# An encoder block on one core: the order of Down's loads, of the norm2 transposes and of the first loads of x

## The chip, the core and the metric

The kernel is one launch on one core of a Trainium2 chip. The core has a matrix engine (TensorE, "PE" in the profile, its weight loads "PEld"), a vector engine (DVE), a scalar engine (ACT), GpSimd (POOL) and a queue engine (SP) that only issues DMAs. POOL also issues some DMAs. Each engine runs its own instructions strictly in the order in which the program lists them; semaphores tie the engines together. The metric is device time in microseconds (us), lower is better.

## The reference, cut to what matters

```
def reference(x, ...):                      # x: 1 x 1024 rows x 1024 channels, float32
    xn = rmsnorm(x, norm1)
    x  = x + token_mixer(xn, ...)           # mLSTM (4 heads, two directions) and
                                            # differential attention (8 heads):
                                            # y = sigmoid(ga)*(h_a @ p_a) + sigmoid(gb)*(h_b @ p_b)
                                            # return y @ w_o
    x  = x + conv_ffn(rmsnorm(x, norm2), ...)
def conv_ffn(xn, w_up, conv_w, conv_b, w_down):
    u = conv3(xn @ w_up) + conv_b           # 1024 -> 5632 channels, 3 taps along the rows
    a, g = split(u, 2)
    return (gelu(g) * a) @ w_down           # 2816 -> 1024
def rmsnorm(x, g): return x * rsqrt(mean(x*x) + 1e-6) * g
```

## The kernel before

All arithmetic is float32. For the matrix engine each operand is split into a high part (rounded to the engine's fp32r) and a low remainder, and a product is three matmuls, high x high, low x high, high x low (`mm3`, lines 101 to 103). The high part is a cast on ACT (L81), the low part a subtraction on DVE (L83) or POOL (L88). So every tile that enters a product costs ACT and DVE or POOL an instruction before PE may start.

The stages, in the order in which PE meets them:

1. **Start.** x is loaded in eight blocks of 128 rows (512 KB each), in two halves of four blocks: half 0 on SP's queue, half 1 on POOL's queue (L273). `norm_transpose` normalises a half: square with a row sum on ACT (L233), scale and add on DVE (L220), power -1/2 on POOL (L221), scaling of the rows on DVE (L236). Then PE transposes the rows in 128 x 128 pieces (L242), ACT evicts them as high part (L243) and DVE as low part (L244) of xn, and the first projections (tile `pj`) follow.
2. **mLSTM**, **attention** and **merge**, not touched by the change.
3. **w_o** (tile `sm`, weights `whi`/`wlo`, left operand `y`, 128 x 256 pieces). `wo_piece` multiplies two blocks of rows with 256 columns: 48 matmuls, and DVE adds the residual (L985). The first twelve of sixteen pieces complete rows 0 to 3 (of eight blocks). `norm0` then normalises these four blocks (`rows(0, ...)`: squares L1049, L220, L221, scaling L1055), transposes them (`turn`, L1061) into the blocks A11 and A12, and evicts each transposed piece three times: high part on ACT (L1076), low part on DVE (L1077), an unsplit copy `f` on ACT (L1078). Then come the last four w_o pieces, for rows 4 to 7, and norm1, the same for these rows.
4. **Up**: x1n @ w_up by a Strassen-Winograd scheme with seven products for each of 22 column blocks j, then the convolution, GELU and gate. The results go to DRAM: `h_d` 0 and 1 by POOL's queue (L1238, L1240), the pair sums `h_d` 2 and 3, formed by DVE (L1251 to L1254), by SP's queue (L1255, L1256).
5. **Down**: the same scheme, seven products n = 0..6, each over 11 steps kk. A step needs a 512-wide piece of h (`hr`, loaded in pairs of kk, L1336) and of w_down (`wd`: n = 0 loads the even row blocks, n = 1 the odd ones, L1304), splits both (`dh` on ACT, `dl` on DVE) and runs 12 matmuls. For n = 1, 2 and 6 DVE forms weight sums first (L1323 to L1328). `x1r` is the residual (L1367).

Tiles live in rings: a tag names a ring with a fixed count of buffers, and a new tile waits for the last user of the buffer that it takes. The ring "A" holds the blocks A11, A12 and their sums in Up, and then parts of w_down and t3 in Down; "B" and "acc" hold rows, `hr`, `x1r`, and the other part of w_down.

The order on each engine is not the order of the code: a scheduler simulates the program at build time and lists each engine's instructions as they come ready in its own model of time. `tc.issue_after(ins)` adds an edge to this: what is issued inside may not be listed ahead of `ins`.

Of the kernel before, what the change touches and what calls it, by code (L numbers as in the profile page):

```python
# [39 lines left out]
NH = 4  # L40
PRO = 4
LAST = (2, 2, 2, 2, 0, 0, 0, 0)
TURN0 = {1: (0,), 2: (2, 3)}
# [7 lines left out]
class Kern:  # L51
# [46 lines left out]
    def mm3(self, ps, a, b, start, stop, again=False):  # L98

        mm = self.nc.tensor.matmul  # L100
        mm(ps, a[0], b[0], start=start, stop=False, skip_group_check=again)  # L101
        mm(ps, a[0], b[1], start=False, stop=False, skip_group_check=again)  # L102
        mm(ps, a[1], b[0], start=False, stop=stop, skip_group_check=again)  # L103

# [113 lines left out]
def rstd_pow(K, out, ss, n, scr, width):  # L218

    K.nc.vector.tensor_scalar(scr, ss, 1.0 / n, EPS, op0=ALU.mult, op1=ALU.add)  # L220
    K.nc.gpsimd.tensor_tensor(out, scr, K.mhalf[:scr.shape[0], :width], op=ALU.pow)  # L221


def norm_transpose(K, xb, xT, gain, tmp, half, dst, psf):


    nc = K.nc
    xs = []
    for b4 in range(4):
        x = xb(half * 4 + b4)  # L230
        ss = tmp.tile([P, 2], F32, tag="nss", bufs=8, name=K.nm("nss"))
        junk, o = dst(x)
        nc.scalar.activation(junk, x, AF.Square, accum_out=ss[:, 0:1])  # L233
        r = tmp.tile([P, 1], F32, tag="nr", bufs=8, name=K.nm("nr"))
        rstd_pow(K, r, ss[:, 0:1], D, ss[:, 1:2], 1)
        nc.vector.tensor_scalar(o, x, r, None, op0=ALU.mult)  # L236
        xs.append(o)
    t = slice(half * 512, half * 512 + 512)
    for k in range(KT):
        ps = psf(k)  # L240
        for b4 in range(4):
            nc.tensor.transpose(ps[:, b4 * P:(b4 + 1) * P], xs[b4][:, k * P:(k + 1) * P], K.ident)  # L242
        nc.scalar.activation(xT[0][k][:, t], ps, AF.Copy, scale=gain[:, k:k + 1])  # L243
        nc.vector.scalar_tensor_tensor(xT[1][k][:, t], ps, gain[:, k:k + 1],  # L244
                                       xT[0][k][:, t].bitcast(F32), op0=ALU.mult, op1=ALU.subtract)


def mlstm(K, xn, g1, gate_bias, ha_d):
# [4 lines left out]
    with tc.tile_pool(name="ml", bufs=1, reuse_waits="tile") as mp, ExitStack() as es:  # L253
# [23 lines left out]
        def norm(xs, half):  # L277
            norm_transpose(K, lambda blk: xs[blk % 4], xn, g1, mp, half,
                           lambda x: (K.big(), x), lambda k: K.small(tag="cr"))
# [614 lines left out]
def merge_ffn(K, ha_d, hb_d, out):  # L894
    nc, tc, I = K.nc, K.tc, K.I
    V, G, A, T = nc.vector, nc.gpsimd, nc.scalar, nc.tensor
    with tc.tile_pool(name="mf", bufs=1, reuse_waits="tile") as fp, ExitStack() as es:
# [99 lines left out]
        for i in range(2):  # L997
            for bp in range(2):
                wo_piece(ws[i], 2 + i, bp * 2)
        up.norm0([g4("nxs", tag="wk") for _ in range(2)] + [g4("nxs", tag="B") for _ in range(2)], lambda k: K.small())  # L1000
# [8 lines left out]
class Up:  # L1009
# [53 lines left out]
    def norm0(self, scr, psf):  # L1063
        nc, G, V = self.K.nc, self.K.nc.gpsimd, self.K.nc.vector
        xs = self.rows(0, scr)
        self.f = []
        for kk in range(4):
            f = self.g4("f", tag="acc")
            for i, name in enumerate(("11", "12")):
                k = kk + 4 * i  # L1070
                ps = psf(2 * kk + i)
                self.turn(xs, k, ps)
                h, l = self.block(name, kk, "A")
                t = slice(i * 512, i * 512 + 512)
# [4 lines left out]
            self.f.append(f)  # L1079

    def norm1a(self):
# [206 lines left out]
class Down:  # L1288
# [7 lines left out]
    def __init__(self, K, g4, up, out):  # L1296
        self.K, self.g4, self.up, self.out = K, g4, up, out
        self.e, self.o, self.t3 = [None] * self.NK, [None] * self.NK, [None] * self.NK
        self.raw = {}
# [30 lines left out]
    def act(self, n, kk):  # L1330

        if kk % 2 == 0 and (n, kk) not in self.raw:
            (i, c), m = self.ORDER[n][0], min(2, self.NK - kk)
            t = self.g4("hr", tag="B" if n == 0 and kk < 4 else "acc")
            src = self.up.h_d[i][kk * P:(kk + m) * P, c:c + 512]
            self.K.nc.sync.dma_start(t[:, :m * 512].rearrange("p (k t) -> p k t", k=m),  # L1336
                                     src.rearrange("(k p) t -> p k t", p=P))
            self.raw[n, kk] = t
# [22 lines left out]
    def x1(self, th, ch, add):  # L1361
        V, nc = self.K.nc.vector, self.K.nc
        r = []
        for b2 in range(2):
            t = self.g4("x1r", tag="B")
            r0, c = (th * 4 + b2 * 2) * P, slice(ch * 512, ch * 512 + 512)
            nc.sync.dma_start(t.rearrange("p (b c) -> p b c", b=2),  # L1367
                              self.up.x1_d[r0:r0 + 2 * P, c].rearrange("(b p) c -> p b c", p=P))
            for i in range(2):
# [123 lines left out]
```

## Time and profile before

| | |
|---|---|
| median of the runs | 2150.89 us (2146.47, 2150.89, 2152.11) |
| profiled execution, its own time | 2153.54 us |
| span of the profiled execution | 2151.8 us |
| PE busy | 2081.1 us, 97% of the span, 11808 matmuls and transposes |
| DVE, ACT, POOL busy | 1328.1, 961.8, 450.4 us |

The profiled execution's own time is 1.7 us more than its span and 2.65 us more than the median. A row of the waits says how long an engine stood idle in front of instructions of a line, in how many places, and which instruction let it go on. A row of the busy time by stretch gives for each engine the busy time and (xN) the instructions in it, then the granted clock of PE as a share of full speed, the busy share of the DMA engines, and GB/s. PE's instructions overlap, so a matmul's own duration is longer than its distance to the next one.

### The profile page before, as it was taken

The page shows a single profiled execution, that of the slowest core. Times are in us where ns is not written, and L with a number is a line of the kernel's source. Part 1 is how long each engine was busy: PE and PEld are TensorE (multiplying, and loading weights), DVE is VectorE, ACT ScalarE, POOL GpSimd, SP SyncE. Part 2 cuts the span into 40 slices and gives each one's busy share as a digit, 9 for nine tenths or more (in the row PEclk, how much of TensorE's full clock was granted, in tenths as well). Part 3 has the DMA queues.
Part 4 walks back from the last instruction along what each step waited for, and adds up shares of the span by engine and source line. Part 5 has one row for each costly group of instructions (what it writes and reads, how often), then busy time and mean ns, then how long its engine had stood idle before and what let it go on. Part 6 is the DMA issues. An engine that isn't in the chain of part 4 may idle for free.

```text
span 2151.8 us, 30492 instructions
## 1 busy us (share of the span) xinstructions
PE 2081.1 (97%) x11808; PEld 1803.0 (84%) x11808; DVE 1328.1 (62%) x2128; ACT 961.8 (45%) x1781; POOL 450.4 (21%) x557
## 2 busy tenths in 40 slices
PE   7999999999999999999999999999999999998999
PEld 5878889898889888988888888898788888887887
DVE  4356454445586856858666534425987777779554
ACT  4332222234555655645655422205645444544443
POOL 1111000143442624425240010000121222120000
PEclk9999999999999999999999999999999999999999
DMA  4224322153413325233243364512232322358441
GB/s 138 40 85 124 67 71 60 40 137 59 99 45 72 80 59 96 52 84 70 64 95 103 127 212 157 165 42 79 79 111 96 113 98 96 111 192 303 141 137 45
DMA packets 167134, 217.39 MB, mean 101 GB/s; under 512 B 18292, under 2 KB 124996, under 8 KB 166988
## 3 DMA queue, kind: packets, MB, share of 16 engines
q1 hardware_dynamic: 152492, 165.55, 25.9%
q0 software_dynamic: 14496, 49.88, 8.8%
q8 instruction: 93, 1.52, 0.3%
q14 instruction: 53, 0.43, 0.1%
HBM read 149.82 MB, written 48.79 MB: 92 GB/s over the span
## 4 chain that ended last, share of the span: by engine, by line
PE 56%; DMA 2%; DVE 2%; ACT 1%; issue 1%; SPq 0%; POOL 0%; ACTq 0%; DVEq 0%
PE sm L101 13%; PE sm L102 13%; PE sm L103 13%; PE pj L101 3%; PE pj L102 3%; PE pj L103 3%; PE big L688 2%; PE pt L719 1%; DMA kst<-st 1%; PE po L101 1%; PE po L102 1%; PE po L103 1%; DMA hr<-h_d 0%; DMA wd<-in_w_down_dram 0%; PE big L101 0%
## 5 line engine op out<-in xcount | busy, mean ns | idle before, releaser
L101 PE MATMUL pj<-whi,xn 128*128 128x256 f32 x960 | 277.6, 289 | 1.1 <-ACT raw L598 1.1
L102 PE MATMUL pj<-wlo,xn 128*128 128x256 f32 x960 | 274.9, 286 | 0.0
L103 PE MATMUL pj<-whi,xn 128*128 128x256 f32 x960 | 274.6, 286 | 0.0
L101 PE MATMUL pj<-xn,whi 128*128 128x512 f32 x512 | 210.4, 412 | 4.2 <-ACT tg L154 2.0
L102 PE MATMUL pj<-xn,whi 128*128 128x512 f32 x512 | 207.7, 406 | 0.0
L103 PE MATMUL pj<-xn,wlo 128*128 128x512 f32 x512 | 207.0, 404 | 0.0
L101 PEld LDWEIGHTS pj<-whi,xn 128*128 128x128 f32 x960 | 183.5, 191 | 5.3 <-ACT raw L598 2.0
L102 PEld LDWEIGHTS pj<-wlo,xn 128*128 128x128 f32 x960 | 183.3, 191 | 2.2
L103 PEld LDWEIGHTS pj<-whi,xn 128*128 128x128 f32 x960 | 183.3, 191 | 1.1
L694 ACT ACTIVATE p<-big,smx 128x1024 f32<-128x1024 f32 x128 | 143.3, 1120 | 82.4 <-DVE smx L692 69.7
L692 DVE TENSOR_REDUCE smx<-big 128x1 f32<-128x1024 f32 x128 | 154.6, 1217 | 39.6 <-PE big L688 39.1
L81 ACT CAST whi<-wraw 128x1024 fp32r<-128x1024 f32 x88 | 92.2, 1049 | 158.5 <-DMA wraw<-in_w_in_dram 34.9
L1234 POOL TENSOR_TENSOR cv<-cv,cv 128x256 f32<-128x256 f32 x88 | 81.5, 954 | 353.0 <-ACT uh L81 122.9
L688 PE MATMUL big<-kst,qst 128*128 128x512 f32 x512 | 145.3, 403 | 4.6 <-ACT p L694 2.4
L83 DVE TENSOR_TENSOR wlo<-wraw,whi 128x1024 fp32r<-128x1024 f32 x54 | 66.3, 1228 | 129.1 <-ACT whi L81 128.9
L102 PE MATMUL sm<-AS,uh 128*128 128x512 f32 x352 | 138.9, 395 | 0.8 <-DVE AS L83 0.8
L101 PE MATMUL sm<-AS,uh 128*128 128x512 f32 x352 | 138.6, 394 | 0.9 <-ACT AS L81 0.7
L103 PE MATMUL sm<-AS,ul 128*128 128x512 f32 x352 | 137.7, 394 | 1.5 <-DVE ul L83 1.5
L83 DVE TENSOR_TENSOR wTl<-pt,wTh 128x512 fp32r<-128x512 f32 x128 | 87.0, 685 | 80.6 <-ACT wTh L81 80.4
L88 POOL TENSOR_TENSOR wlo<-wraw,whi 128x256 fp32r<-128x256 f32 x136 | 110.7, 845 | 118.6 <-ACT whi L81 118.3
L101 PE MATMUL sm<-dh 128*128 128x512 f32 x308 | 116.1, 393 | 7.3 <-ACT dh L81 7.3
L102 PE MATMUL sm<-dl,dh 128*128 128x512 f32 x308 | 120.3, 392 | 0.0
(311 smaller groups left out, 5308.4 us busy)
## 6 DMA issues: line engine op xcount, KB each, us to landing
ur<-in_w_up_dram SPq DMA_DIRECT2D x88, 256.0 KB, 3.3
hr<-h_d SPq DMA_DIRECT2D x35, 512.0 KB, 3.8
kst<-st SPq DMA_DIRECT2D x128, 128.0 KB, 2.6
wraw<-in_w_in_dram SPq DMA_DIRECT2D x24, 512.0 KB, 5.5
h_d<-cv SPq DMA_DIRECT2D x22, 512.0 KB, 2.6
wd<-in_w_down_dram SPq DMA_DIRECT2D x22, 512.0 KB, 9.8
sig<-tg SPq DMA_DIRECT2D x32, 256.0 KB, 2.3
wraw<-in_w_in_dram POOLq DMA_DIRECT2D x16, 512.0 KB, 6.1
```

The source lines that it names most:

```text
L81: self.nc.scalar.copy(hi, src)
L83: self.nc.vector.tensor_tensor(lo, src, hi.bitcast(F32), op=ALU.subtract)
L88: lo_eng.tensor_tensor(lo[:, t], src[:, t], hi[:, t].bitcast(F32), op=ALU.subtract)
L101: mm(ps, a[0], b[0], start=start, stop=False, skip_group_check=again)
L102: mm(ps, a[0], b[1], start=False, stop=False, skip_group_check=again)
L103: mm(ps, a[1], b[0], start=False, stop=stop, skip_group_check=again)
L688: T.matmul(sps[c_][:, half * 512:half * 512 + 512], o.q[st.qp][:, c_, t], o.k[half][:, c_, s_, :], start=s_ == 0, stop=s_ == 1)
L692: V.tensor_reduce(sm[:, c_:c_ + 1], sp, op=ALU.max, axis=AX.X, negate=True)
L694: K.mark = A.activation(p_, sp, AF.Exp, bias=sm[:, c_:c_ + 1], accum_out=sm[:, 2 + c_:3 + c_]).ins
L719: T.transpose(pt[:, kk * 256 + j * P:kk * 256 + (j + 1) * P], st.w[j][:, kb * P:(kb + 1) * P], K.ident)
L1234: nc.gpsimd.tensor_tensor(a[:, t], a[:, t], g[:, t], op=ALU.mult)
```

## The change

- **Start.** 28 transposes of the identity into the PSUM tile `pj` are issued ahead of everything else on PE. x's half 1 is loaded after the last power of half 0's normalisation, so SP's four blocks come first and alone.
- **norm0** becomes a generator. Rows 0 to 3 are normalised as before, but the transposes are cut in four turns of eight, one after each of the four remaining w_o pieces, and each turn may not be listed ahead of that piece's last matmul.
- **Down.** All loads of Down (`hr`, `wd`, `x1r`) go through `ld`, which keeps them in the order in which the code issues them. Even row blocks of w_down take buffers of ring "A", odd ones of ring "B" (before: the other way round).

```
+WARM = 28
...
+        self.last_mm = mm(ps, a[1], b[0], start=False, stop=stop, skip_group_check=again).ins
...
+    return K.nc.gpsimd.tensor_tensor(out, scr, K.mhalf[:scr.shape[0], :width], op=ALU.pow).ins
...
             if first:
                 xs0 = load_x(0, nc.sync)
+                for i in range(WARM):
+                    if i % 4 == 0:
+                        ps = K.small(tag="pj")
+                    T.transpose(ps[:, i % 4 * P:i % 4 * P + P], K.ident, K.ident)
...
-                norm(xs0, 0)
-                xs1 = load_x(1, G)
+                last = norm(xs0, 0)
+                with tc.issue_after(last):
+                    xs1 = load_x(1, G)
...
-        up.norm0([g4("nxs", tag="wk") ...], lambda k: K.small())
+        turns = up.norm0([g4("nxs", tag="wk") ...], lambda k: K.small())
+        next(turns)
         for i in range(2):
             for bp in range(2):
                 wo_piece(ws[i], 2 + i, 4 + bp * 2)
+                next(turns)
...
         self.f = []
+        yield
         for kk in range(4):
...
-                self.turn(xs, k, ps)
+                with self.K.tc.issue_after(self.K.last_mm):
+                    self.turn(xs, k, ps)
...
+    def ld(self, dst, src):
+        if self.last is None:
+            self.last = self.K.nc.sync.dma_start(dst, src).ins
+        else:
+            with self.K.tc.issue_after(self.last):
+                self.last = self.K.nc.sync.dma_start(dst, src).ins
...
-        t = self.g4("wd", tag="A" if k % 2 else "B")
-        K.nc.sync.dma_start(t, K.I["w_down"][0][k * P:(k + 1) * P, :])
+        t = self.g4("wd", tag="B" if k % 2 else "A")
+        self.ld(t, K.I["w_down"][0][k * P:(k + 1) * P, :])
...
-            self.K.nc.sync.dma_start(t[:, :m * 512]...)        # hr, and x1r likewise
+            self.ld(t[:, :m * 512]..., ...)
```

Line numbers of the changed kernel are 1 higher from line 42, some 8 higher from line 290 and 10 to 20 higher behind that.

POOL's instructions at the start (`nr` the power of half 0's four blocks, `x` the loads of half 1), before:

```order
L273 DMA x_217<-in_x_dram 128x1024
L273 DMA x_219<-in_x_dram 128x1024
L273 DMA x_221<-in_x_dram 128x1024
L273 DMA x_223<-in_x_dram 128x1024
L221 TENSOR_TENSOR nr_136<-nss_133,mhalf 128x1
L221 TENSOR_TENSOR nr_143<-nss_140,mhalf 128x1
L221 TENSOR_TENSOR nr_150<-nss_147,mhalf 128x1
L221 TENSOR_TENSOR nr_157<-nss_154,mhalf 128x1
```

and after the change:

```order
L222 TENSOR_TENSOR nr_171<-nss_168,mhalf 128x1
L222 TENSOR_TENSOR nr_178<-nss_175,mhalf 128x1
L222 TENSOR_TENSOR nr_185<-nss_182,mhalf 128x1
L222 TENSOR_TENSOR nr_192<-nss_189,mhalf 128x1
L275 DMA x_252<-in_x_dram 128x1024
L275 DMA x_254<-in_x_dram 128x1024
L275 DMA x_256<-in_x_dram 128x1024
L275 DMA x_258<-in_x_dram 128x1024
```

The four loads of half 1 move behind the four powers, each of which waits for a block of half 0.

PE at the w_o pieces, where rows 0 to 3 are turned (`nxs` normalised rows). Before, the end of one piece and the first of 32 transposes, which stand in one row:

```order
L101 MATMUL sm_13981<-whi_13807,y_12796 128x256
L102 MATMUL sm_13981<-wlo_13808,y_12796 128x256
L103 MATMUL sm_13981<-whi_13807,y_12804 128x256
L1061 MATMUL sm_14065<-ident,nxs_14032 128x128
L1061 MATMUL sm_14075<-ident,nxs_14032 128x128
L1061 MATMUL sm_14086<-ident,nxs_14032 128x128
L1061 MATMUL sm_14094<-ident,nxs_14032 128x128
```

After the change, the end of the last piece, the fourth turn and the first product of Up (`A`, `uh`, `ul`):

```order
L103 MATMUL sm_14311<-wlo_13843,y_12835 128x256
L104 MATMUL sm_14311<-whi_13842,y_12843 128x256
L1071 MATMUL sm_14363<-ident,nxs_14067 128x128
L1071 MATMUL sm_14363<-ident,nxs_14068 128x128
L1071 MATMUL sm_14363<-ident,nxs_14069 128x128
L1071 MATMUL sm_14363<-ident,nxs_14070 128x128
L1071 MATMUL sm_14371<-ident,nxs_14067 128x128
L1071 MATMUL sm_14371<-ident,nxs_14068 128x128
L1071 MATMUL sm_14371<-ident,nxs_14069 128x128
L1071 MATMUL sm_14371<-ident,nxs_14070 128x128
L102 MATMUL sm_14428<-A_2146_14156,uh_14379 128x512
L103 MATMUL sm_14428<-A_2147_14157,uh_14379 128x512
```

The other three turns stand in the same way behind the first three of the last four pieces (of the first turn, two transposes stand nine matmuls into the next piece); nothing stands now between the piece that completes rows 0 to 3 and the next piece's matmuls.

SP at the seam of Up and Down, before (the last four of eleven `wd` loads in a row, then two `x1r`, then the `hr` of kk = 4):

```order
L1304 DMA wd_17871<-in_w_down_dram 128x1024
L1304 DMA wd_17893<-in_w_down_dram 128x1024
L1304 DMA wd_17913<-in_w_down_dram 128x1024
L1304 DMA wd_17935<-in_w_down_dram 128x1024
L1367 DMA x1r_18141<-x_d 128x2x512
L1367 DMA x1r_18145<-x_d 128x2x512
L1336 DMA hr_17807<-h_d 128x2x512
```

After the change (from the `hr` of kk = 2 to the `hr` of kk = 6; the two `h_d` are the stores of an earlier pair):

```order
L1320 DMA hr_17800<-h_d 128x2x512
L1320 DMA wd_17802<-in_w_down_dram 128x1024
L1320 DMA wd_17822<-in_w_down_dram 128x1024
L1268 DMA h_d<-cv_17538 128x1024
L1269 DMA h_d<-cv_17398 128x1024
L1320 DMA hr_17842<-h_d 128x2x512
L1320 DMA wd_17844<-in_w_down_dram 128x1024
L1320 DMA wd_17864<-in_w_down_dram 128x1024
L1320 DMA hr_17884<-h_d 128x2x512
```

Each `hr` now stands directly ahead of the `wd` of its own two steps; the `hr` of kk = 10 is row 332 of SP, `x1r` and the odd blocks come behind it.

DVE at the same seam after the change (`dl` the low parts of Down's steps kk = 5 to 7, L1264 to L1266 the pair sums of the last pair of Up):

```order
L84 TENSOR_TENSOR dl_17867<-wd_17864,dh_17866 128x512
L84 TENSOR_TENSOR dl_17889<-hr_17884,dh_17888 128x512
L1264 TENSOR_TENSOR cv_17758<-cv_17682,cv_17763 128x512
L84 TENSOR_TENSOR dl_17909<-hr_17884,dh_17908 128x512
L1265 TENSOR_TENSOR cv_17758<-cv_17758,cv_17682 128x512
L1266 TENSOR_TENSOR cv_17682<-cv_17682 128x512
L84 TENSOR_TENSOR dl_17889<-wd_17886,dh_17888 128x512
L84 TENSOR_TENSOR dl_17909<-wd_17906,dh_17908 128x512
```

Before the change the weight sums of n = 1 (L1323 to L1326) stood among these rows, fifteen of them ahead of PE's stop; now all 44 stand behind the last `dl` of n = 0.

## Rows read from the trace of the kernel before

**Rows 1.** PE's line of the profile page: busy, share, instructions, of all engines.

```profile
PE 2081.1 (97%) x11808; PEld 1803.0 (84%) x11808; DVE 1328.1 (62%) x2128; ACT 961.8 (45%) x1781; POOL 450.4 (21%) x557
```

**Rows 2.** Waits of PE over the whole span: for, total us, times, longest us.

```profile
PE cr L242 <- DVE x L236: 13.7, 2, 12.3
...
PE sm L101 <- ACT dh L81: 7.3, 1, 7.3
...
PE cr L461 <- DVE dn L476: 3.9, 1, 3.9
```

**Rows 3.** ACT in order of time at the start, first and last square of half 0.

```profile
7.42 1.03 ACT L233 ACTIVATE big<-x 128x1024 f32<-128x1024 f32 x1 [5.03 <-DMA x<-in_x_dram]
...
15.45 1.03 ACT L233 ACTIVATE big<-x 128x1024 f32<-128x1024 f32 x1 [1.51 <-DMA x<-in_x_dram]
```

**Rows 4.** Busy time by stretch at the start: PE, PEld, DVE, ACT, POOL, clock, DMA, GB/s.

```profile
8.00:12.00 4.00, 0.00 (x0) 0.00 (x0) 0.74 (x3) 1.71 (x4) 0.92 (x2) 1.00 1.03 422
```

**Rows 5.** PE in order of time at the start.

```profile
12.31 1.12 PE L242 MATMUL cr<-ident,x 128*128 128x128 f32 x4 [12.31 <-DVE x L236]
...
19.51 1.22 PE L101 MATMUL pj<-xn,whi 128*128 128x512 f32 x2
```

**Rows 6.** PE's groups by form, 21.5 to 26.2 us.

```profile
L101 PE MATMUL pj<-xn,whi 128*128 128x512 f32 x2 | 1.3, 628 | 0.0
```

**Rows 7.** PE's groups by form, 28 to 36 us.

```profile
L101 PE MATMUL pj<-xn,whi 128*128 128x512 f32 x9 | 3.3, 405 | 0.0
```

**Rows 8.** Busy time by stretch around a wait of the mLSTM.

```profile
128.00:132.00 4.00, 0.84 (x8) 0.64 (x6) 3.20 (x4) 1.64 (x2) 1.09 (x1) 1.00 0.37 146
132.00:136.00 4.00, 3.25 (x9) 2.69 (x9) 1.94 (x8) 1.91 (x4) 1.09 (x1) 0.57 0.00 0
```

**Rows 9.** Waits of PE, 1455 to 1520 us.

```profile
PE sm L101 <- ACT f L1078: 2.3, 1, 2.3
PE sm L1061 <- DVE nss L220: 1.6, 1, 1.6
PE sm L103 <- DVE ul L83: 1.5, 1, 1.5
```

**Rows 10.** PE in order of time at norm0.

```profile
1460.23 1.91 PE L1061 MATMUL sm<-ident,nxs 128*128 128x128 f32 x16
```

**Rows 11.** DVE in order of time at norm0, scaling of the fourth block.

```profile
1464.37 0.75 DVE L1055 TENSOR_SCALAR nxs<-x,nr 128x1024 f32<-128x1024 f32 x1 [0.66 <-POOL nr L221]
```

**Rows 12.** Busy time by stretch around norm0 and the first products of Up.

```profile
1462.00:1470.00 8.00, 3.73 (x29) 3.12 (x28) 5.29 (x10) 5.54 (x11) 1.10 (x2) 1.00 0.29 115
1470.00:1480.00 10.00, 10.00 (x87) 10.00 (x86) 3.21 (x6) 6.04 (x11) 0.00 (x0) 1.00 0.01 2
1500.00:1520.00 20.00, 16.69 (x71) 12.13 (x70) 19.93 (x33) 14.34 (x27) 0.00 (x0) 1.00 0.19 56
```

**Rows 13.** SP's queue in order of time, 1880 to 1952 us.

```profile
1921.50 9.98 SPq L1304 DMA_DIRECT2D wd<-in_w_down_dram  x11
...
1935.60 4.30 SPq L1336 DMA_DIRECT2D hr<-h_d  x4
```

**Rows 14.** Busy time by stretch at PE's stop in front of Down.

```profile
1930.00:1940.00 10.00, 9.35 (x41) 7.32 (x39) 7.05 (x10) 5.01 (x6) 0.00 (x0) 1.00 1.02 412
1940.00:1942.00 2.00, 0.00 (x0) 0.00 (x0) 2.00 (x3) 0.00 (x0) 0.00 (x0) 0.84 1.04 388
1942.00:1950.00 8.00, 3.33 (x8) 2.66 (x9) 5.28 (x10) 3.74 (x7) 3.65 (x5) 0.50 1.05 395
```

**Rows 15.** POOL in order of time, 1925 to 1947 us.

```profile
1926.05 0.60 POOL L1238 DMA_DIRECT2D h_d<-cv  x1
1942.29 3.08 POOL L1234 TENSOR_TENSOR cv<-cv,cv 128x256 f32<-128x256 f32 x4 [15.64 <-issue]
```

**Rows 16.** Busy time by stretch in Down's product n = 1.

```profile
1970.00:1980.00 10.00, 10.00 (x46) 8.29 (x45) 10.00 (x17) 4.19 (x8) 0.00 (x0) 1.00 0.58 181
1990.00:2000.00 10.00, 10.00 (x46) 8.29 (x45) 6.91 (x12) 4.57 (x8) 0.00 (x0) 1.00 0.27 92
```

More of the change, by code (lines that the diff above doesn't have):

```diff
@@ L102, in mm3 @@
         mm(ps, a[0], b[1], start=False, stop=False, skip_group_check=again)
-        mm(ps, a[1], b[0], start=False, stop=stop, skip_group_check=again)
+        self.last_mm = mm(ps, a[1], b[0], start=False, stop=stop, skip_group_check=again).ins
     def proj_cm(self, ps, w, c0, x, half):
@@ L220, in rstd_pow @@
     K.nc.vector.tensor_scalar(scr, ss, 1.0 / n, EPS, op0=ALU.mult, op1=ALU.add)
-    K.nc.gpsimd.tensor_tensor(out, scr, K.mhalf[:scr.shape[0], :width], op=ALU.pow)
+    return K.nc.gpsimd.tensor_tensor(out, scr, K.mhalf[:scr.shape[0], :width], op=ALU.pow).ins
 def norm_transpose(K, xb, xT, gain, tmp, half, dst, psf):
@@ L234, in norm_transpose @@
         r = tmp.tile([P, 1], F32, tag="nr", bufs=8, name=K.nm("nr"))
-        rstd_pow(K, r, ss[:, 0:1], D, ss[:, 1:2], 1)
+        last = rstd_pow(K, r, ss[:, 0:1], D, ss[:, 1:2], 1)
         nc.vector.tensor_scalar(o, x, r, None, op0=ALU.mult)
@@ L245, in norm_transpose @@
                                        xT[0][k][:, t].bitcast(F32), op0=ALU.mult, op1=ALU.subtract)
+    return last
 def mlstm(K, xn, g1, gate_bias, ha_d):
@@ L277, in norm @@
         def norm(xs, half):
-            norm_transpose(K, lambda blk: xs[blk % 4], xn, g1, mp, half,
+            return norm_transpose(K, lambda blk: xs[blk % 4], xn, g1, mp, half,
                            lambda x: (K.big(), x), lambda k: K.small(tag="cr"))
@@ L999, in merge_ffn @@
                 wo_piece(ws[i], 2 + i, bp * 2)
-        up.norm0([g4("nxs", tag="wk") for _ in range(2)] + [g4("nxs", tag="B") for _ in range(2)], lambda k: K.small())
+        turns = up.norm0([g4("nxs", tag="wk") for _ in range(2)] + [g4("nxs", tag="B") for _ in range(2)], lambda k: K.small())
+        next(turns)
         for i in range(2):
@@ L1079, in norm0 @@
             self.f.append(f)
+            yield
     def norm1a(self):
@@ L1298, in __init__ @@
         self.e, self.o, self.t3 = [None] * self.NK, [None] * self.NK, [None] * self.NK
-        self.raw = {}
+        self.raw, self.last = {}, None
+    def ld(self, dst, src):
[4 more added lines that the diff above has]
+                self.last = self.K.nc.sync.dma_start(dst, src).ins
     def load_w(self, k):
         K = self.K
-        t = self.g4("wd", tag="A" if k % 2 else "B")
-        K.nc.sync.dma_start(t, K.I["w_down"][0][k * P:(k + 1) * P, :])
+        t = self.g4("wd", tag="B" if k % 2 else "A")
+        self.ld(t, K.I["w_down"][0][k * P:(k + 1) * P, :])
         (self.o if k % 2 else self.e)[k // 2] = t
@@ L1335, in act @@
             src = self.up.h_d[i][kk * P:(kk + m) * P, c:c + 512]
-            self.K.nc.sync.dma_start(t[:, :m * 512].rearrange("p (k t) -> p k t", k=m),
-                                     src.rearrange("(k p) t -> p k t", p=P))
+            self.ld(t[:, :m * 512].rearrange("p (k t) -> p k t", k=m), src.rearrange("(k p) t -> p k t", p=P))
             self.raw[n, kk] = t
@@ L1366, in x1 @@
             r0, c = (th * 4 + b2 * 2) * P, slice(ch * 512, ch * 512 + 512)
-            nc.sync.dma_start(t.rearrange("p (b c) -> p b c", b=2),
-                              self.up.x1_d[r0:r0 + 2 * P, c].rearrange("(b p) c -> p b c", p=P))
+            self.ld(t.rearrange("p (b c) -> p b c", b=2), self.up.x1_d[r0:r0 + 2 * P, c].rearrange("(b p) c -> p b c", p=P))
             for i in range(2):
```

## Prediction

> **What bounds the kernel now.** The page comes first: PE is busy for 2081.1 us, 97% of the span [rows 1], so the span is PE's work plus 2151.8 - 2081.1 = 70.7 us of gaps, and a change that leaves the products alone can only win gaps, or time in which PE runs at half its clock. Next the waits of PE [rows 2]: the largest entries are 13.7 us at the first transposes, 7.3 us for one high part `dh`, and 3.9 us once for `dn` in the mLSTM. The first two, and a group of smaller ones at norm0, are where the change works. Last come order of time and stretches of these three places.
>
> At the start ACT squares x's first block at 7.42 and the fourth at 15.45 [rows 3], one block each (15.45 - 7.42) / 3 = 2.7 us, although 422 GB/s arrive [rows 4], at which 0.524 MB take 1.24 us. Half 0 and half 1 share the bandwidth, and PE needs only half 0 to begin; its first product stands at 19.51 [rows 5]. From 21.5 to 26.2 a 128 x 512 product lasts 628 ns [rows 6], from 28 on 405 [rows 7]. The granted clock reads 1.00 there all the same, so here I go by durations: they are those of the half level, 1.2 GHz, against 2.4. That a stop of PE brings the half level is seen where the record does show it: PE is busy 0.84 of 4 us at 128, and the next 4 us have a granted clock of 0.57 [rows 8].
>
> At norm0 PE waits 1.6 us for row sums and 2.3 for the evictions of the transposes [rows 9]. It has started 16 of the 32 transposes at 1460.23 [rows 10], and the last normalised block is scaled from 1464.37 to 1465.12 [rows 11]. From 1462 to 1470 it is busy 3.73 of 8.00 us: 4.27 us lost. The clock stays 1.00. Behind that, 1500 to 1520, it loses 3.31 us while DVE is busy 19.93 of 20 [rows 12].
>
> In front of Down SP issues eleven `wd` loads from 1921.50 on and reaches the `hr` of kk = 4 at 1935.60 [rows 13]. The DMA engines are full (412 GB/s), so the tile lands late, and PE stands for the 7.3 us; the granted clock is 0.84, then 0.50 [rows 14].
>
> **The change, part by part.** The products are the same. Added on PE: 28 transposes, before any x is there.
>
> *x by halves.* Alone, SP's first block needs 1.24 us instead of twice that: its square starts at about 7.42 - 1.24 = 6.2, the fourth at 6.2 + 3 x 1.24 = 9.9, so 15.45 - 9.9 = 5.5 us earlier, and the chain behind it (square, sum, power, scaling, transposes, eviction) is unchanged. First product near 14.0. Half 1 is issued by POOL behind the fourth power, near 12, in the shadow of the first projections; POOL has nothing else to do there. Cover: some 15 us of products on half 0. If these loads come late, PE waits at the second half's projections instead, at worst the same 5.5 us. The bounds are 4 us (ACT and DVE get half 0's work and the splits of the weights closer together, which may cost a microsecond and a half) and 5.5.
>
> *Idle transposes.* They end long before x is there (four transposes take 1.12 us [rows 5], so 28 take 7.8 us, from about 2 on). Should PE then be at its full level and keep it over gaps of about 1 us between x's blocks, as it did over the gaps at norm0 [rows 12], the products between 21.5 and 26.2 run at the full level: matmuls 0.43 us apart against 0.23, so 4.7 us become 2.5, a gain of 2.2. If not, 0. Nothing is lost, PE was idle. No row shows a raise by transposes, so I take the middle, 1.1. Start: 5.5 + 1.1 = 6.5 rounded, ends 4 and 8.
>
> The Trainium skill, "TensorE: Matmul & The Clock Gate", Part 4 (PE-mode transpose), says that the full clock does not engage for transposes, which do not count as a busy PE in the same way. By that the term is 0 and the start gains 5.5. No row here speaks against it: the transposes at norm0 that ran at 1.00 came directly behind products.
>
> *Turns between w_o pieces.* After the piece that completes rows 0 to 3, 48 matmuls at 10 / 87 = 0.115 us follow, 5.5 us, so the first turn is due at 1460.23 + 5.5 = 1465.8, and the last scaling ends at 1465.12: covered by 0.7 us. Each turn of 8 transposes asks ACT for four evictions and DVE for two, at about 6.04 / 11 = 0.55 us [rows 12], so 2.2 and 1.1 us in the 5.5 of a piece: no wait. The 4.27 us go. What is late next: the fourth turn stands directly in front of Up's first product, and its low parts queue on DVE among Up's `ul`, of which one already costs 1.5 us [rows 9]; I give 0.7 us back. 3.5 us, bounds 2 and 4.3.
>
> *Down's loads.* The `hr` of kk = 4 now has the loads of kk = 0 to 3 and no others ahead of it, so the 7.3 us go, and with them the half level: 15 matmuls between 1942 and 1952 took 3.33 + 2.0 us instead of 15 x 10 / 46 = 3.3, so 2.0 us; together about 9.4. The same loads move elsewhere: the odd blocks and `x1r` come behind the `hr` of kk = 10, needed only in n = 1, 29 us later, and even blocks use ring "A". The weight sums, fifteen of which DVE did ahead of the stop, all fall into n = 1. There 60 instructions of DVE stand between its first and last low part; at 10 / 17 = 0.59 us [rows 16] that is 35 us against PE's 11 x 12 x 10 / 46 = 29. DVE can bring the 6 us along from n = 0, where it needs 22 x 0.59 = 13 us of 29, but not more than the four buffers of `dh` allow, 4 x 2.6 = 10. I take 1.4 us for what is late: 8 us, bounds 5 (a wait as in the second rival) and 9.7.
>
> Between these places the order is the same, apart from one or two products of filler in the first mLSTM head, which I price at -1 to +1.
>
> Sum: 6.5 + 3.5 + 8 = 18.0, ends 11 and 22. The profiled execution took 2153.5, so 2135.5 in its frame; it lies 2.65 above the median of the runs, so 2132.9: **2133 us**, the likeliest case's own range 2128 to 2140.
>
> **The rivals.**
>
> 1. *The idle transposes do nothing* (or the clock falls again before 14). Against the gaps of about a microsecond stand [rows 12], for it the 16 transposes at the start, behind which the products ran at the half level [rows 6]. Gain 17: 2134.
>
> 2. *DVE becomes the bound in Down.* Either the pair sums: POOL's last pass ended at 1942.29 + 3.08 = 1945.4 [rows 15], and a low part of kk = 6 now stands behind L1264, which waits for it. PE begins kk = 4 where it stopped before, at 1930 + 9.35 = 1939.35 [rows 14], and kk = 6 at 1939.35 + 2 x 2.6 = 1944.6. Five instructions of DVE from 1945.4 on end at 1948.3: a wait of 3.7 us, if POOL comes no earlier. Or n = 1 with no lead, 6 us. For it: DVE 10.00 of 10 [rows 16]. Against: 3.09 us of DVE idle 20 us later, and POOL's pass waits for convolutions which DVE did behind weight sums that are gone. Gain 18 - 3.7 to 18 - 6: 2137 to 2139.
>
> 3. *Given back in the mLSTM.* PE comes to the wait for `dn` 6.5 us earlier; if that chain does not start earlier, the start's gain is waited off there: 2139.5. Against: everything in it hangs on xn. With rival 2 on top, 2145, no change to be seen. Norm0 may fail likewise, if the evictions come late in DVE's full stretch at 1500: 3.5 less, 2136.5.
>
> 4. *Slower: SP's one order.* Each load waits on SP for its buffer and its source, and holds all behind it. The `hr` of kk = 10 needs POOL's store of `h_d`, issued at 1926.05 [rows 15]. The tile that ended PE's stop took from 1935.60 to 1939.35 + 7.3 = 1946.65, 11 us, to land and be split [rows 13, 14]; by that the store has landed by 1937. Behind it stand the odd blocks, which n = 1 wants from 1939.35 + 7 x 2.6 = 1957.6 on. With 11 us for themselves, SP must be past this point by 1946. Each us beyond costs one, and a stop of several also some 2 us at half level. It is slower than before by over 0.3% only from 18 + 6.5 - 2 = 22 us beyond, SP held until 1968: from there on 2158 and more. Against: nothing in the trace holds a store for so long.
>
> 5. *Less of it happens than said*: x's half 1 comes late and Down's stop only moves to another load (the DMA engines stay full, [rows 14]). Gain 5.5 to 3.5 or less: 2145 to 2150.
>
> **How the numbers follow.** Forecast 0.45 (2128 to 2140), rival 1 0.20, rival 2 0.13, rival 3 0.09, rival 4 0.05, rival 5 0.08. About 0.3%, 6.5 us, is what a measurement can tell from no change, so faster means below 2144.4: all of the forecast and rivals 1 and 2, two thirds of rival 3, none of 5: 0.45 + 0.20 + 0.13 + 0.06 = 0.84; within 0.3%: 0.03 + 0.08 = 0.11; slower 0.05. The range goes from 2126 (all ends at their best, 22 us, and a filler that helps) to 2146, which leaves out rival 4, most of rival 5 and some of the best end.
>
> **What would show it.** Right: ACT's fourth square near 10 and the first product near 14, with 512-wide products at about 400 ns from then on (at about 630 until after 20, rival 1); no wait of PE for `f` (L1090 of the changed kernel) and 10.00 of 10 us around 1465; no PE wait above 2 us at the seam, granted clock 1.00 there. Wrong: a PE wait for `dl` behind L1264 or in n = 1 (rival 2), a longer wait for `dn` (rival 3), a DMA as releaser of `dh` in n = 0 or 1 with SP's queue held (rivals 4 and 5).

## The result, and the profile after

| | before | after |
|---|---|---|
| median (lowest to highest), us | 2152.11 (2146.47 to 2158.73) | 2138.21 (2136.70 to 2141.92) |
| ratio to before, 95% interval | | 0.994 (0.9922 to 0.9959) |
| profiled execution, us | 2153.5 | 2141.92 |

The change makes the kernel faster by 0.6%: 13 us, by the interval 9 to 17. The total lies in the predicted range. Its terms do not: one of the three gave nothing, one gave half of what was forecast, one more.

To price the terms apart the trace is cut at three instructions that both kernels have: the first subtraction for the gate weights on DVE (end of "start"), the first square of norm0's rows on ACT, and the first convolution of Up on DVE. The last stage ends with the last matmul. Lengths in us, each from one trace; "again" is a second trace of the same kernel:

| | start | mLSTM, attention, merge | norm0 | Up and Down |
|---|---|---|---|---|
| before | 61.46 | 1393.74 | 75.89 | 616.36 |
| before again | 61.41 | 1392.21 | 77.09 | 616.81 |
| after | 61.63 | 1391.01 | 70.65 | 612.58 |
| after again | 61.10 | 1383.64 | 70.63 | 612.58 |

Start: 0.1 us gained by the two means (61.44 to 61.37); in five variants below that keep after's order there it ends at 60.22 to 61.76. norm0: 5.9. Up and Down: 4.0. Together 10. What is left of the 13 lies in the second column, which the change does not touch; it varies by 7 us between two traces of one kernel, more than there is to explain.

The page's line of busy times of after answers to [rows 1]:

```profile
PE 2084.3 (97%) x11836; PEld 1805.5 (84%) x11836; DVE 1325.5 (62%) x2128; ACT 961.0 (45%) x1781; POOL 450.0 (21%) x557
```

PE has the 28 transposes more, and 2140.2 - 2084.3 = 55.9 us of gaps in place of 70.7. The waits of PE over the span of after answer to [rows 2] (waited for, total us, times, longest us):

```profile
PE pj L102 <- ACT xn L244: 5.0, 3, 3.0
...
PE cr L243 <- DVE nss L221: 4.5, 3, 2.8
...
PE cr L469 <- DVE dn L484: 4.0, 1, 4.0
PE sm L103 <- DVE dl L84: 3.8, 4, 1.7
```

The 13.7 us for x and the 7.3 for `dh` are gone; at the same transposes 4.5 us for `nss` remain (1.1 before). Two entries are new: 5.0 us for `xn` at the start, which no step of the prediction had, and 3.8 us for `dl`, which its second rival had. `dn` is as before.

ACT in order of time at the start of after, the rows that answer to [rows 3] and those behind them (start, length, instruction, and in brackets the idle time before it with what ended it):

```profile
6.46 1.03 ACT L234 ACTIVATE big<-x 128x1024 f32<-128x1024 f32 x1 [4.07 <-DMA x<-in_x_dram]
...
10.46 1.03 ACT L234 ACTIVATE big<-x 128x1024 f32<-128x1024 f32 x1 [0.18 <-DMA x<-in_x_dram]
...
16.21 1.04 ACT L82 CAST whi<-wraw 128x1024 fp32r<-128x1024 f32 x1 [2.99 <-DMA wraw<-in_w_in_dram]
17.16 1.26 ACT L244 ACTIVATE xn<-cr,g 128x512 fp32r<-128x512 f32 x2
22.80 1.03 ACT L234 ACTIVATE big<-x 128x1024 f32<-128x1024 f32 x1 [4.38 <-DMA x<-in_x_dram]
...
28.05 1.05 ACT L82 CAST whi<-wraw 128x1024 fp32r<-128x1024 f32 x1 [1.92 <-DMA wraw<-in_w_in_dram]
```

The fourth square is 5.0 us earlier, as forecast. But ACT works its list in order. The evictions `xn`, for which PE waits, stand behind a cast that waits 2.99 us for weights (16.21), then behind the first square of half 1, which waits 4.38 us for x (22.80), then behind a cast that waits 1.92 us (28.05). PE in order of time in the same stretch answers to [rows 5]:

```profile
1.50 4.97 PE L290 MATMUL pj<-ident 128*128 128x128 f32 x28 [1.50 <-POOL ident masks.py:199]
9.30 0.66 PE L243 MATMUL cr<-ident,x 128*128 128x128 f32 x4 [2.82 <-DVE nss L221]
...
12.27 1.11 PE L243 MATMUL cr<-ident,x 128*128 128x128 f32 x4 [0.83 <-DVE nss L221]
...
17.90 1.22 PE L102 MATMUL pj<-xn,whi 128*128 128x512 f32 x2 [3.04 <-ACT xn L244]
```

The 28 transposes do raise the clock: the first x transposes behind them take 0.66 us for four, in place of 1.12 [rows 5]. Behind gaps of 2.82, 0.83 and 0.83 us it is lost again: the third four take 1.11. Stretches of after from 8 us on (columns as in [rows 4]):

```profile
8.00:12.00 4.00, 1.31 (x8) 0.84 (x8) 2.17 (x5) 3.31 (x6) 1.56 (x3) 0.98 0.96 309
12.00:16.00 4.00, 2.23 (x8) 1.43 (x8) 2.16 (x4) 1.05 (x1) 3.06 (x5) 0.50 0.61 99
16.00:20.00 4.00, 1.99 (x7) 1.27 (x7) 2.55 (x3) 2.21 (x3) 0.00 (x0) 0.50 0.46 172
```

The granted clock is 0.98, then 0.50 in front of the first product. From 12 to 20 us the DMA engines move only 99 and 172 GB/s while ACT waits for them.

Now norm0 and two places of Down, the stretches that answer to [rows 12, 16]:

```profile
1452.00:1472.00 20.00, 20.00 (x172) 20.00 (x171) 9.74 (x22) 9.99 (x18) 2.23 (x4) 1.00 0.27 106
1970.00:1980.00 10.00, 8.37 (x36) 6.29 (x35) 10.00 (x18) 2.77 (x5) 0.00 (x0) 1.00 0.42 133
1990.00:2000.00 10.00, 8.26 (x37) 6.52 (x36) 10.00 (x17) 3.43 (x6) 0.00 (x0) 1.00 0.38 141
```

At norm0 PE is full. Down's n = 1 runs from 1952.3 to 1984.5 us in after (in before from 1968.2 to 1998.1), so the second of these rows is in n = 1 and the third already in n = 2. PE has gaps in both, where [rows 16] have none, and DVE is full. The first gap comes in n = 0. PE, DVE and POOL of after in order of time, one to three rows of each:

```profile
1933.46 0.50 PE L103 MATMUL sm<-dl,dh 128*128 128x512 f32 x1 [1.00 <-DVE dl L84]
```

```profile
1931.58 0.69 DVE L84 TENSOR_TENSOR dl<-hr,dh 128x512 fp32r<-128x512 f32 x1
1932.19 2.36 DVE L84 TENSOR_TENSOR dl<-wd,dh 128x512 fp32r<-128x512 f32 x2
1934.47 1.22 DVE L84 TENSOR_TENSOR dl<-hr,dh 128x512 fp32r<-128x512 f32 x1
```

```profile
1931.82 4.47 POOL L1247 TENSOR_TENSOR cv<-cv,cv 128x256 f32<-128x256 f32 x4 [12.29 <-ACT dh L82]
```

While POOL adds (1931.82 to 1936.3), three low parts take 1.2 us each on DVE, in place of 0.69 just before, and PE waits. That POOL's addition slows them is a reading: no run moves it, and elsewhere most of DVE's instructions beside it are not slowed (last section).

### The profile page after: what moved, and what is told of

Read it like the earlier page. It is cut to its first block, busy times and chain, and to the rows that moved or that the text cites. A ratio compares the mean times of both kernels' runs of the same rounds, so it can differ in the third digit from the quotient of the medians.

```text
span 2140.2 us, 30556 instructions
## 1 busy us (share of the span) xinstructions
PE 2084.3 (97%) x11836; PEld 1805.5 (84%) x11836; DVE 1325.5 (62%) x2128; ACT 961.0 (45%) x1781; POOL 450.0 (21%) x557
## 3 DMA queue, kind: packets, MB, share of 16 engines
q1 hardware_dynamic: 152492, 165.55, 26.2%
## 4 chain that ended last, share of the span: by engine, by line
PE 54%; DVE 3%; DMA 1%; ACT 1%; issue 1%; SPq 0%; POOL 0%; ACTq 0%; DVEq 0%
PE sm L103 12%; PE sm L104 12%; PE sm L102 12%; PE pj L102 3%; PE pj L103 3%; PE pj L104 3%; PE big L696 3%; PE pt L727 1%; PE po L102 1%; PE po L103 1%; PE po L104 1%; DMA kst<-st 1%; DMA hr<-h_d 1%; DVE dl L84 1%; PE big L102 0%
## 5 line engine op out<-in xcount | busy, mean ns | idle before, releaser
L1247 POOL TENSOR_TENSOR cv<-cv,cv 128x256 f32<-128x256 f32 x88 | 81.8, 958 | 350.4 <-ACT uh L82 122.8
L103 PE MATMUL sm<-AS,uh 128*128 128x512 f32 x352 | 138.9, 395 | 0.8 <-DVE AS L84 0.8
L102 PEld LDWEIGHTS pj<-xn,whi 128*128 128x128 f32 x512 | 96.9, 190 | 32.6 <-ACT xn L244 6.3
```

The costliest lines, as they stand in the source:

```text
L1247: nc.gpsimd.tensor_tensor(a[:, t], a[:, t], g[:, t], op=ALU.mult)
```

## The experiments

Each is an edit of the changed kernel, except the two repetitions. Ratios are to before, with their 95% interval; "after again" is 0.9941 (0.9926 to 0.9955).

**The start: idle transposes left out.**

```
-WARM = 28
+WARM = 0
```

> The changed kernel without the 28 idle transposes. Theory: they raise the clock from about 4 us on, but it is back at the half level from 11 to 22 us, when the first products run, so nothing of it reaches them: time within 1 us of the changed kernel (about 0.994 of before), transposes of x's blocks 0.28 us apart instead of 0.11, first product still at about 17.9 us because it waits for an ACT eviction behind a weight cast. Rival (they win what was forecast): 1 to 2 us slower than the changed kernel, about 0.995.

Measured: 0.9947 (0.993 to 0.9963), 2141.3 us; start 61.85 us. PE at the start:

```profile
9.06 1.11 PE L243 MATMUL cr<-ident,x 128*128 128x128 f32 x4 [9.06 <-DVE nss L221]
...
16.58 1.22 PE L102 MATMUL pj<-xn,whi 128*128 128x512 f32 x2 [1.96 <-ACT xn L244]
```

Without them the x transposes run at the half level from the first on, and the first product is no later (16.58; after again has 16.67). The start is 0.1 us longer than the longest of the traces that have them (61.76) and 0.8 longer than the mean of these seven (61.0). So the 2.2 us that a clock kept up would have given are not there; whether they are worth nothing or up to 0.8 us, one trace does not tell. The median, 1.6 to 3.1 us above those of after, does not decide it either: the intervals overlap.

**The start: half 1 of x loaded at once.** POOL issues it first, as before the change.

```
-                with tc.issue_after(last):
-                    xs1 = load_x(1, G)
+                xs1 = load_x(1, G)
```

> The changed kernel with half 1 of x loaded at once, as before, the idle transposes kept. Theory (the start is bound by the weight loads and ACT's fixed order, not by x): within 1.5 us of the changed kernel, PE first product 1 to 2 us later (near 19.5), but fewer waits from 22 to 32, since half 1 is there for its squares; no change from 60 us on. Rival (x by halves wins the 5.5 us forecast): 4 to 5 us slower, about 0.996 of before.

Measured: 0.9969 (0.9957 to 0.9981), 2144.8 us. The first product is at 19.67, near the 19.51 before the change, and the start still takes 61.32 us: so x by halves brings the product forward and the stage nothing. The 5 us by which the total is worse lie elsewhere, against the expectation that nothing changes from 60 us on: Up and Down take 617.49. The edit at the start also changed the order in Up and Down, in many places of PE and DVE. At kk = 4 of n = 0 PE now waits for low parts that DVE does behind two convolutions (from 1927.73) and beside POOL's addition. PE and its stretch there:

```profile
1933.26 0.50 PE L103 MATMUL sm<-dl,dh 128*128 128x512 f32 x1 [2.76 <-DVE dl L84]
```

```profile
1930.00:1940.00 10.00, 7.24 (x26) 5.47 (x25) 9.38 (x14) 2.74 (x6) 5.02 (x5) 0.83 0.82 272
```

A wait of 2.76 us and a granted clock of 0.83 behind it. The total of this run prices the new order, not the edit.

**The start: ACT's order.** The second cast waits behind the second eviction, the later casts and half 1's squares behind the last eviction of half 0 (`K.ev`, the evictions).

```
+                wqk = Weights(K, src); wqk.load(0); wqk.make(0); wqk.load(1)
...
+                wqk.make(1, K.ev[1])
...
+                wv = K.load_w([...], after=evl if first else None)
...
-                    norm(xs1, 1)
+                    norm(xs1, 1, evl)
```

> The changed kernel with ACT's order at the start alone: second weight cast behind the second eviction of half 0, half 1's squares and the value weights' casts behind its last eviction; half 1 still loaded by POOL behind the fourth power. Theory: first product near 15.5 us, half 0's evictions done by 22, then one wait of 2 to 4 us for the value weights or for half 1's first block near 26 to 28, because these loads land when they did; row table 1 to 3 us earlier than in the changed kernel. Rival (the loads bind): row table within 0.7 us of 101 to 103.

Measured: 0.9942 (0.9927 to 0.9957), 2139.4 us, not apart from after. The mark that ends the start comes at 59.22 us, 2.2 earlier than the mean of after, but this edit moves that subtraction forward among its neighbours: DVE's next low part of weights starts at 63.36, in after at 63.54 and 63.02. The mark that was named before the run, ACT's copy of `cT`, tells the same, first after, then this run:

```profile
102.90 0.40 ACT L420 COPY cT<-cr 128x288 f32<-128x288 f32 x1 [3.28 <-PE cr L418]
```

```profile
102.48 0.40 ACT L434 COPY cT<-cr 128x288 f32<-128x288 f32 x1 [3.99 <-PE cr L432]
```

After again has 102.38, and the five variants with the same order 101.49 to 103.03. So the start is not shorter, and the rival's case is the one that came. ACT, then PE:

```profile
27.98 1.05 ACT L82 CAST whi<-wraw 128x1024 fp32r<-128x1024 f32 x1 [4.81 <-DMA wraw<-in_w_in_dram]
```

```profile
14.64 1.22 PE L102 MATMUL pj<-xn,whi 128*128 128x512 f32 x2
...
31.93 0.63 PE L248 MATMUL cr<-ident,x 128*128 128x128 f32 x4 [2.96 <-DVE x L241]
```

The first product is now at 14.64, near the 14.0 of the forecast, with no wait for `xn` on half 0. But then ACT stands 4.81 us for the value weights, with half 1's squares behind the cast. Another wait for a load has taken the place of the first, at the same price.

**The start: half 1 on SP, behind the first weights.**

```
-                with tc.issue_after(last):
-                    xs1 = load_x(1, G)
+                xs1 = load_x(1, nc.sync)
```

> The changed kernel with half 1 of x loaded by SP directly behind half 0 and the first weights, instead of by POOL behind the fourth power; from the second head of the mLSTM on every engine's order is that of the changed kernel. Theory (at the start ACT stands 4 to 6 us for half 1's first block, which comes 10 us after POOL issues it, and half 0's evictions stand behind its square): ACT's wait before that square falls below 2 us, PE's waits for evictions between 22 and 32 us go, and the first 128 x 256 product comes 2 to 4 us earlier (near 35). If PE's work is all that bounds the stretch up to 120 us, the time falls by as much, to about 0.9925 of before. Rival (the mLSTM's first chunk waits on something that starts with a load and not with xn): the early gain is gone at the wait for dn, which still ends near 132.5, and the time is that of the changed kernel.

Measured: 0.9945 (0.9925 to 0.9966), 2141.8 us; start 59.19 us, 2.2 less than the mean of after and 1.0 less than the lowest of the seven traces with its order there; `cT` is copied at 100.37. ACT:

```profile
16.78 1.04 ACT L82 CAST whi<-wraw 128x1024 fp32r<-128x1024 f32 x1 [3.82 <-DMA wraw<-in_w_in_dram]
...
18.31 1.02 ACT L234 ACTIVATE big<-x 128x1024 f32<-128x1024 f32 x1
```

The wait for half 1 is gone, the one for the weights stays. The gain is kept through the mLSTM: PE's wait for `dn` ends at 130.37, in after at 132.85 and 132.60 (131.22 the lowest of the seven). So the start's gain is not waited off there. The total does not show it; the profiled execution, 2148.4 us, spent 1400.21 in the middle stage.

**norm0: the 32 transposes in one row again.**

```
-        next(turns)
+        for _ in turns:
+            pass
...
-                with self.K.tc.issue_after(self.K.last_mm):
-                    self.turn(xs, k, ps)
+                self.turn(xs, k, ps)
```

> The changed kernel with the 32 transposes of norm0 in a row again, as before. Theory: the waits of 1.6, 0.4 and 2.3 us at norm0 return and the time goes up by 4.3 to 5.2 us, to about 0.9965 of before. Rival (the 2.5 us by which the changed kernel's trace is already ahead at 1450 us are part of it, and norm0 gives only 2.7): up by 2 to 3 us.

Measured: 0.9981 (0.9969 to 0.9993), 2149.0 us. norm0 takes 76.98 us, as in the two traces of before, so the turns are the whole of that term. Its waits are those of [rows 9]; here the granted clock falls behind them (stretch of this run, from 1.6 us after the last of them):

```profile
1460.00:1462.00 2.00, 2.00 (x11) 2.00 (x11) 0.52 (x2) 2.00 (x5) 0.00 (x0) 0.50 0.00 0
```

Up and Down take 617.00, with a wait for `dl` of 2.75 us at the same step as with the early x, so again the total is not the edit's price.

**Down: both halves of its change undone, then each alone.** The first diff is the order, the second the rings; "both" has the two.

```
-        if self.last is None: ... else: with self.K.tc.issue_after(self.last): ...
+        self.K.nc.sync.dma_start(dst, src)
```

```
-        t = self.g4("wd", tag="B" if k % 2 else "A")
+        t = self.g4("wd", tag="A" if k % 2 else "B")
```

Both undone:

> The changed kernel with Down's loads free of order again and w_down's even and odd blocks in the old rings; start and norm0 as changed, and every instruction up to the last column block of Up in the same order. Theory (Down's part wins the stop of 7.3 us and its half level, but pays about 4.6 us in waits for low and high parts behind DVE): 4 us slower than the changed kernel, about 0.996 of before, with one wait of PE of 5 to 9 us for a high part whose tile comes late, and no waits in n = 1. Rival (Down's part wins all of the 8 us forecast and the shortfall is only noise): 8 us slower, about 0.998.

Rings undone, the order kept:

> The changed kernel with only the rings swapped back (even blocks of w_down in ring B, odd ones in A), the loads still in one order. Theory (the order of the loads is what removes the stop; the ring decides when a load may be issued): even blocks wait for ring B, which is freed later, so SP holds its one order at an even block and PE waits again at kk = 4 to 8 of n = 0: 2 to 6 us slower than the changed kernel. Rival (the ring makes no difference): within 1 us.

Order undone, the new rings kept:

> The changed kernel with only the fixed order of the loads taken away, the new rings kept. Theory (the order is what counts): loads of odd blocks and of x1r stand ahead of the hr tiles of n = 0 again, PE waits for a high part there, 3 to 8 us slower than the changed kernel. Rival (the rings alone do it): within 1 us, and since odd blocks come earlier, DVE does weight sums earlier and the waits in n = 1 shrink: up to 3 us faster.

Measured: 0.9954 (0.9936 to 0.9972); 0.9958 (0.9941 to 0.9975); 0.9966 (0.9951 to 0.9982). Up and Down: 615.84, 617.23, 618.84 us, in after 612.58. The totals are hardly apart from each other and from after; the verdict rests on the stage and its waits. All waits of PE in Up and Down, in this order:

```profile
PE sm L102 <- ACT dh L82: 7.4, 1, 7.4
```

```profile
PE sm L103 <- DVE dl L84: 6.7, 5, 3.9
```

```profile
PE sm L102 <- ACT dh L82: 6.0, 1, 6.0
PE sm L103 <- DVE dl L84: 1.4, 1, 1.4
PE sm L104 <- DVE dl L84: 0.7, 1, 0.7
```

Each half alone leaves as much waiting as none. The order alone ends the stop for `dh` but makes DVE late by 6.7 us; its price is the expected one, but not its wait, which was to be for a held load. The rings alone keep most of the stop. Both undone cost the stage 3.3 us: the theory's 4, not the rival's 8.

**Down: the sums of n = 2 and 6 later.** In each step the weight sums `t2` and `t4` may not come ahead of the last low part asked for, so low parts go first on DVE.

```
+            self.last_lo = self.nc.vector.tensor_tensor(lo, ...).ins
...
+            with self.K.tc.issue_after(self.K.last_lo):
                 V.tensor_tensor(w("t2", kk), ...)
...
+            with self.K.tc.issue_after(self.K.last_lo):
                 V.tensor_tensor(w("t4", kk), ...)
```

> The changed kernel with the weight sums that n = 2 and n = 6 need held back: each may not be listed ahead of the low part of the step before the one that needs it. DVE then has 47 instructions in n = 1 instead of 62. Theory (DVE is the bound in n = 1 and n = 2, and holds PE for the 3.8 us of waits for low parts and 0.8 for a high part): the waits between 1945 and 2000 us go, 2.5 to 3.6 us faster than the changed kernel, about 0.9925 of before; the wait of 1.0 us at 1932 stays. Rival (the waits come from the loads, which the low parts wait for): no change, the waits stay, with a DMA as what DVE waits for.

Measured: 0.9912 (0.9894 to 0.9931), 2134.1 us; Up and Down 608.54 us, 4.0 less than after and 8.0 less than before, which is Down's forecast. The waits of PE there, then two stretches:

```profile
PE sm L103 <- DVE dl L84: 1.3, 2, 1.0
```

```profile
1970.00:1980.00 10.00, 10.00 (x45) 8.07 (x44) 9.43 (x17) 3.59 (x7) 0.00 (x0) 1.00 0.44 157
...
1990.00:2000.00 10.00, 10.00 (x46) 8.29 (x45) 7.17 (x12) 4.79 (x9) 0.00 (x0) 1.00 0.36 125
```

PE is full where it had gaps. DVE has the same sums to do, only later.

**All three:** half 1 on SP, ACT's order, the later sums.

> The changed kernel with three things on top: half 1 of x on SP's queue behind the first weights; at the start the second weight cast behind the second eviction of half 0, and half 1's squares and the value weights' casts behind its last eviction; the weight sums of n = 2 and n = 6 held back. Theory (the start is bound by ACT's fixed order, in which an eviction stands behind a cast or a square that waits for a load): first product near 15.5 us, no wait of PE above 1 us from there to 26, the row table (ACT's copy of cT) 3 to 5 us earlier than in the changed kernel (97 to 99 us), the wait for dn ending near 129, no waits for low parts in Down's n = 1 and n = 2; 7 to 8 us faster than the changed kernel, about 0.990 of before. Rival (the loads themselves bound the start, whatever ACT's order): first product earlier, but PE then waits for the value weights, row table not before 100 us, time that of the kernel with late sums alone, 0.9912.

Measured: 0.9891 (0.9872 to 0.9911), 2126.4 us, better than both kernels: 12 us below after, 26 below before. norm0 takes 70.39 us, Up and Down 609.26. For the start the copy of `cT` is again the mark:

```profile
98.37 0.40 ACT L433 COPY cT<-cr 128x288 f32<-128x288 f32 x1 [3.99 <-PE cr L431]
```

That is 4.3 us earlier than the mean of after (102.64). PE at the start:

```profile
14.63 1.22 PE L102 MATMUL pj<-xn,whi 128*128 128x512 f32 x2
...
31.31 0.39 PE L102 MATMUL pj<-whi,xn 128*128 128x256 f32 x1 [1.88 <-ACT qT L318]
```

Between these rows PE has no wait. By this mark the edits of the start are worth 0.2 us (ACT's order, within the scatter) and 2.3 (half 1 on SP) alone and 4.3 together: each alone leaves the other's wait standing in the same list. The start and Down account for some 8 of the 12 us; the rest lies in the middle stage, whose scatter is as large.

**Before and after once more,** for the scatter of the stages.

> The kernel before once more, for a second trace. Every theory: a time of 2147 to 2158. Theory (the attention stage differs by several us from one execution to the next, since the clock falls at some of its waits and not at others): the stretch from the end of the wait for dn to the first w_o residual differs from 1268.5 us by 2 us or more, with the start, norm0 and Down within 1 us of the first trace. Rival (the changed kernel is really faster there): 1268 again.

> The changed kernel once more, for a second trace and a narrower interval. Theory: 0.994 to 0.995 of before; norm0's stretch (first w_o residual to first convolution) 125.4 us and Down's (first convolution to the last product) 612.6 within 0.5 us of the first trace; start within 1.3 us, since the landing of the first weights moves; attention differing by 2 us or more. Rival: the stretches of norm0 and Down move too, and the gain by stretch cannot be read from one trace.

Measured: 2153.6 us for before, 2139.6 us for after, 0.9941 (0.9926 to 0.9955). The start, norm0, Up and Down agree within 1.2 us in two traces of one kernel. The middle stage differs by 7.4 us between the two of after, as expected; between the two of before it differs by 1.5, less than the 2 that were expected (table above).

## Why the prediction was right, and where it was wrong

**Start, forecast 6.5, measured about 0: wrong.** "The chain behind it (square, sum, power, scaling, transposes, eviction) is unchanged" is the step that failed. The squares came as forecast; the eviction is not only behind the transposes, it is behind whatever stands ahead of it on ACT. Before the change half 0 was the last to arrive: behind the fourth square [rows 3] ACT waits for no load in the next 12 us. With half 0 early, the second cast, half 1's squares and the value weights' cast became the late ones, 9.3 us of waiting on ACT, of which PE sees 5.0. "At worst the same 5.5 us" was the right bound for it, but as a bound for the loss it belonged in the sum's range: "ends 4 and 8" left it out. The experiments with ACT's order and with half 1 on SP show both waits: taken away one at a time they give 0.2 and 2.3 us, together 4.3.

**Idle transposes, 1.1 of the 6.5, measured 0.** Rival 1's case held, by its second condition: "the clock falls again before 14" (0.50 from 12 us on). The 0 is what one trace shows, to within 0.8 us.

**norm0, forecast 3.5, measured 5.9, above its upper bound of 4.3.** The mechanism is right: PE is full, and the 4.27 us of [rows 12] are gone. Two sizes were off. The 0.7 us given back did not occur: the wait for `ul` is 1.5 us as in [rows 9], the others too. And the waits are not the whole loss. From the first square to Up's first product it takes 36.3 us in the trace of before, 37.5 in the second one, 31.2 in both of after: 5.1 and 6.3 us, where the waits account for 4.3. In the second trace, and in the experiment with one row of transposes, the half level follows the stop; that is the 1.2 us between the two. The 0.8 us that is left was not taken apart.

**Down, forecast 8, measured 4.0, below its lower bound of 5.** "The 7.3 us go, and with them the half level" held: no stop, granted clock 1.00. The mis-sized term is the 1.4 us for DVE: PE waits 3.8 us for `dl` and 0.8 for `dh`. This is rival 2, whose price was 3.7 to 6. Both places it named occur: 1.3 us in n = 0 beside POOL's pass, where low parts take 1.2 us in place of 0.69, and 1.6 in n = 1, where DVE is full. The longest single wait, 1.7 us at 1995.4, is in n = 2, which it did not name. The rate of 0.59 us held in n = 1 (10.00 us for 18 instructions, POOL idle). What failed is the lead: low parts stand behind weight sums that only n = 2 and n = 6 need. The experiment with later sums shows it: the same work in another order takes 4.0 us off. A small slip besides: "15 matmuls between 1942 and 1952" counts two twice that lie across 1950; 13 begin there, and the half level cost 2.5 us, not 2.0.

**Rivals 3, 4 and 5.** The wait for `dn` is 4.0 us in place of 3.9 [rows 2], and the experiment with half 1 on SP came to its end 2.5 us earlier, so nothing was waited off in the mLSTM. SP's order held up no product: in n = 0 and 1 of after neither PE nor ACT waits for a load, where before ACT's `dh` waited 6.4 us for `hr`. Of rival 5, the half on the start is what happened, by ACT's list and not by bandwidth alone.

**The sum.** 0 + 5.9 + 4.0 = 10 where 18 was forecast and 13 (9 to 17) measured. The total is nearer the forecast than its terms, in part because norm0's error has the other sign, in part for about 3 us that the stages touched do not show. The middle stage was 1392 to 1394 in both traces of before and 1383 to 1391 in both of after, but also 1400 with half 1 on SP. The first head's filler is not the cause. Up to norm0 the orders differ only ahead of PE's 1200th matmul (idle transposes not counted), near 242 us; from the copy of `cT` to there before takes 139.0 and 138.9 us, after 139.2 and 138.4. From there to norm0's first square PE, ACT, DVE and POOL have the same instructions in the same order in all fourteen traces, and this stretch took 1213.6 and 1212.2 us in before and 1202.8 to 1219.5 in the others. Whether before is really the longer one there, two traces of it do not tell.

## What to carry to other kernels

A load brought forward moves the wait to the next load in the same engine's list: before pricing the gain, list for each engine in order what stands ahead of the instruction that PE needs, and when each of their inputs lands. When a stop of PE goes, the work that other engines did during the stop comes due beside the products; let what the next product needs go ahead of sums that are due later. Compare stages between fixed instructions before reading a total as the price of an edit, since a small edit may change the order far away; and take a second mark further on, since an edit may also move the first one among its neighbours.

## What was not expected of the hardware

- Transposes raise TensorE's clock. Stretches of after, through the 28 transposes:

```profile
1.50:3.00 1.50, 1.50 (x7) 1.50 (x8) 0.00 (x0) 0.88 (x2) 0.08 (x3) 1.00 0.56 4
3.00:4.50 1.50, 1.50 (x9) 1.50 (x8) 0.17 (x1) 0.00 (x0) 0.00 (x0) 1.00 1.10 195
4.50:6.00 1.50, 1.50 (x14) 1.50 (x13) 0.00 (x0) 0.00 (x0) 0.00 (x0) 1.00 1.01 369
```

  7 in the first 1.5 us, 14 in the third: half level, then full. The Trainium skill, "TensorE: Matmul & The Clock Gate", Part 4 (PE-mode transpose), says that the full clock does not engage for them; this trace says otherwise for f32 transposes of 128x128 that stand alone ahead of everything (it lists them as MATMUL and does not show the mode).
- At the start the granted clock reads 1.00 over durations of both levels, in the same stretch as these. It falls to 0.50 only later, between 8 and 16 us; without the idle transposes the x transposes of 9 to 14 us have durations of the half level at a reading of 1.00.
- Half 1 of x, four loads of 512 KB issued by POOL at 12.85 us beside SP's loads of weights, had its first block ready for ACT only at 22.80; the median from issue to landing was 11.0 us.
- In the trace of after none of DVE's 711 TENSOR_TENSOR instructions of 128x512 with no TENSOR_TENSOR of POOL beside them takes over 0.7 us. Of the 26 that lie wholly beside POOL's additions (L1247), 19 take 0.7 as well and five take 1.2. What tells these apart no run shows.
